# The opening of a one-core encoder step: bias rows, first squares, first two projections

## The chip, the cores and the metric

One core of one Trainium2 chip. The metric is device microseconds of one execution of the whole program; before the change three runs took 1292.07 us in the median (1292.02 to 1293.26).

## The reference, cut to what matters

One layer of a streaming encoder, for a prompt of 2048 frames with 16 meta tokens in front and for 32 new frames of a running stream. All in float32:

```
n = rmsnorm(x) * norm_g                      # mean square over 1024 columns
q, k, v, z_a, b_g, c_g, u, z_c = split(n @ w_in)      # 8 x 512 columns
s = q k / 8 + rel_bias[bucket(k_pos - q_pos)]         # 4 heads, two halves each
a = softmax(s1) - lambda * softmax(s2);  o = a @ v    # chunks of 64 frames
y = [rmsnorm(o) * silu(z_a), silu(z_c) * b_g * conv3(c_g * u)] @ w_out
out = rmsnorm(x + y)
```

The bias depends on the distance alone, so each head has one row of 383 values, of which every key window is a shifted copy.

## The kernel before, in words

Each float32 matrix product is made of three matmuls on rounded halves: `xh`/`xl` are the high and low half of a slice of x transposed (128 of the 1024 model columns by up to 560 frames), `wh`/`wl` those of the weights. A column block of 128 projected columns takes 8 slices x 3 matmuls per PSUM bank. The work runs in four passes of 512 frames; pass 0 also holds the 16 meta and 32 sample frames, 560 columns in all, so a column block needs two banks of 272 or 280 columns and 48 matmuls. Within a pass come four heads (`unit_a`: columns CQ, CK, CV, CZ, then `attend`), with the convolution columns (`unit_c`: CC, CU, CB, CG) between them; the output projection ends the program.

PSUM has eight banks: `ps_j` (tag `pj`, 2, for projections), `ps_s` (tag `s`, 3, for attention scores), `ps_t` (2) and `ps_o` (1). In pass 0 the CV block already uses banks of `ps_s`; every other block uses `ps_j`. A bank comes free when VectorE (DVE) has multiplied it by `rbs[p]` into SBUF (`ev_q`, `ev_k`, `ev_v`, `ev_z`: "evacuation" here).

`rbs[0]`, 1/rms of every frame, comes from `x_load(0)`. For each slice k it loads x (tile `g`), makes `xh[k]` on ScalarE (ACT, line 152), `xl[k]` on VectorE (line 153) and the square of the slice (tiles named `ks`, borrowed). Slices 0, 2 and 4 are squared on GpSimd (POOL, line 78, in two halves) and summed there, the other five on ScalarE (line 158) and summed on VectorE (line 162). Then a float32 matmul with a matrix of ones (line 171, `pss`) adds both sums over the partitions, in two halves of 280 frames, and `rsqrt` (lines 178 to 184) makes `rb` of each half: VectorE, two ScalarE steps, four VectorE steps.

`bias_rows` makes the bias row of each head on all 128 partitions by a matmul with a broadcast column (line 601, four of them, in `ps_j`) and a ScalarE copy (`bvec`, line 603). `prep_small` writes each to DRAM (`bd`), reads it back skewed (`g<-bd`), adds the chunk mask on VectorE (line 615), and stores it (`bz`); it also makes lambda (lines 618 to 638).

All DMAs are issued by SP in one order. A scheduler places every instruction, from its own model of times, so a change in one place moves others; each engine then runs its list strictly in that order. The order beyond the first 1300 of 7021 matmuls (about the first 140 us) is the same in both kernels.

Of the kernel before, what the change touches and what calls it, by code (L numbers as in the profile page):

```python
# [11 lines left out]
F32 = mybir.dt.float32  # L12
F32R = mybir.dt.float32r
AF = mybir.ActivationFunctionType
ALU = mybir.AluOpType
AX = mybir.AxisListType

P = 128
D = 1024
KT = D // P  # L20
# [5 lines left out]
H = 4  # L26
# [7 lines left out]
LV = WIN + P - 1  # L34
NP = (12, 6)
# [12 lines left out]
def hybrid_step(ctx: ExitStack, tc: tile.TileContext, x, xT, ckT, cv, scT, rel_bias, norm_g, w_in,  # L48
# [8 lines left out]
    pp = pool("pp", 1)  # L57
# [83 lines left out]
    def x_load(p):  # L141
        c0 = 0 if p == 0 else NX + QT * p
        tw = NX + QT if p == 0 else QT
        if p == 0:
            acc = [None, None]
        for k in range(KT):
            xt = g_tile(tw) if p == 0 else one.tile([P, QT], F32, tag="xt", name="xt", bufs=XB)
            dma(xt, xT[P * k:P * (k + 1), c0:c0 + tw])
            xh[k] = xp.tile([P, NX + QT], F32R, tag=f"xh{k}", name=f"xh{k}")
            xl[k] = xp.tile([P, NX + QT], F32R, tag=f"xl{k}", name=f"xl{k}")  # L150
            with tc.high_priority():
                S.activation(xh[k][:, :tw], xt, AF.Copy, scale=ng[:, k:k + 1])
                V.scalar_tensor_tensor(xl[k][:, :tw], xt, ng[:, k:k + 1], f32(xh[k][:, :tw]),  # L153
                                       op0=ALU.mult, op1=ALU.subtract)
            if p == 0:
                i = (1, 0, 1, 0, 1, 0, 0, 0)[k]
                sq = sqt(k, tw)
                (halved(sq, xt, xt, ALU.mult) if i else S.activation(sq, xt, AF.Square))
                if acc[i] is None:
                    acc[i] = sq  # L160
                else:
                    (G if i else V).tensor_tensor(acc[i], acc[i], sq, op=ALU.add)
        if p == 0:
            rb = one.tile([P, NX + QT], F32, tag="rb", name="rb")
            for i in range(2):
                c = slice(280 * i, 280 * (i + 1))
                var, w = (pp.tile([P, 512], F32, tag="p1", name="xv", bufs=NP[1])[:, :280] for _ in range(2))
                ps = ps_t.tile([P, 2, 256], F32, tag="pt", name="pss").rearrange("p a b -> p (a b)")[:, :280]
                parts = [a[:, c] for a in acc if a is not None]
                for j, a in enumerate(parts):  # L170
                    T.matmul(ps, lhsT=ones, rhs=a, start=(j == 0), stop=(j == len(parts) - 1))
                with tc.high_priority():
                    rsqrt(rb[:, c], ps, var, w, 1.0 / D)
            rbs[0] = rb
# [34 lines left out]
    def proj(col, p, evac):  # L209
        w2 = pre.pop((col, p), None) or w_load(col, p)  # L210
        if p > 0:
            blks = [(0, QT)]
        elif col < CK or CZ <= col < CC or col >= CG:
            blks = [(NM, 288), (288, 560)]
        else:
            blks = [(0, 280), (280, 560)]
        for b0, b1 in blks:
            if p == 0 and col == CV:
                ps = ps_s.tile([P, 512], F32, tag="s", name="pj")[:, :b1 - b0]
            else:  # L220
                ps = ps_j.tile([P, 512], F32, tag="pj", name="pj")[:, :b1 - b0]
            for k in range(KT):
                wh, wl = w2[k // 4]
                for i, (a, b) in enumerate(((wh, xh), (wh, xl), (wl, xh))):
                    T.matmul(ps, lhsT=a[:, k % 4], rhs=b[k][:, b0:b1],  # L225
                             start=(k == 0 and i == 0), stop=(k == KT - 1 and i == 2))
            evac(ps, b0, b1)


# [364 lines left out]
    def bias_rows():  # L594
        rbt = const.tile([32, H], F32, name="rbt")
        dma(rbt, rel_bias)
        oh = pp.tile([P, 512], F32, tag="p1", name="oh", bufs=NP[1])[:32, :LV]
        dma(oh, ohd)
        for h in range(H):
            pv = ps_j.tile([P, 512], F32, tag="pj", name="pv")[:, :LV]  # L600
            T.matmul(pv, lhsT=rbt[:, h:h + 1].broadcast_to([32, P]), rhs=oh, start=True, stop=True)
            bvec = pp.tile([P, 512], F32, tag="p1", name="bvec", bufs=NP[1])[:, :LV]
            S.activation(bvec, pv, AF.Copy, scale=-1.0)
            bvs.append(bvec)

    def prep_small():
        for h in range(H):
            bd = dram.tile([P, LV + 1], F32, name=f"bd{h}", tag=f"bd{h}")
            dma(bd[:, :LV], bvs[h])
            w = g_tile(512)  # L610
            G.memset(w[:, :512 - WIN], 0.0)
            src = bd[:, :]
            toep = bass.AP(tensor=src.tensor, offset=src.offset + P - 1, ap=[[LV, P], [1, WIN]])
            dma(w[:, 512 - WIN:], toep)
            V.tensor_scalar(w[:64, 448:], w[:64, 448:], -NEG, None, op0=ALU.add)
            bzd.append(dram.tile([P, 512], F32, name=f"bz{h}", tag=f"bz{h}"))
            dma(bzd[h], w)
# [195 lines left out]
```

## Time and profile before

| | |
|---|---|
| runs | 1292.02, 1292.07, 1293.26 us |
| the profiled execution | 1293.26 us, of it the span 1291.5 us |
| PE (matmul) busy | 1267.5 us, 98% |
| DVE, ACT, POOL busy | 923.9, 827.5, 699.0 us |
| mean granted clock of TensorE | 0.995 |

Busy is the sum of an engine's instructions; matmuls overlap in the records, so the distance between two starts says more than one duration. "Idle before <- X" names what ended a wait.

### The profile page before, as it was taken

How to read it: one execution, taken by the hardware profiler on the slowest of the kernel's cores; microseconds unless marked ns; L12 is line 12 of the kernel's file. 1: busy time of each engine (PE TensorE's matmuls, PEld its weight loads, DVE VectorE, ACT ScalarE, POOL GpSimd, SP SyncE). 2: the span in 40 equal slices, each digit the busy share in tenths (PEclk: the TensorE clock that was granted, in tenths of full speed). 3: DMA queues.
4: the chain of work that ended last, by engine and by line, in shares of the span. 5: the costliest groups of instructions: out<-in, count | busy, mean ns of one | idle time of the engine just before them, and what ended most of it. 6: DMA issues, size and time to landing. Idle time of an engine off the chain costs nothing.

```text
span 1291.5 us, 21630 instructions
## 1 busy us (share of the span) xinstructions
PE 1267.5 (98%) x7058; PEld 1101.4 (85%) x7058; DVE 923.9 (72%) x2086; ACT 827.5 (64%) x2030; POOL 699.0 (54%) x918
## 2 busy tenths in 40 slices
PE   8999999999999998999999999999999999999897
PEld 6999999988888886888888888888888888888675
DVE  8767566567886847787878677767786896856654
ACT  6745454675776647677767567777777786763322
POOL 5775857767565675455556555364656483432200
PEclk9999999999999999999999999999999999999999
DMA  9834444774445347444343453344334543557652
GB/s 290 226 116 129 141 112 116 216 241 149 137 117 159 125 145 228 156 137 134 101 169 124 142 177 114 116 147 119 117 109 141 177 133 124 177 181 237 215 181 81
DMA packets 108048, 198.74 MB, mean 154 GB/s; under 512 B 17408, under 2 KB 45600, under 8 KB 107936
## 3 DMA queue, kind: packets, MB, share of 16 engines
q1 hardware_dynamic: 107936, 197.37, 49.0%
q8 instruction: 55, 0.90, 0.3%
q14 instruction: 57, 0.47, 0.1%
HBM read 145.62 MB, written 43.26 MB: 146 GB/s over the span
## 4 chain that ended last, share of the span: by engine, by line
PE 55%; DVE 3%; DMA 3%; ACT 1%; issue 1%; DVEq 0%; SPq 0%; ACTq 0%
PE pj L225 27%; PE po L693 9%; PE s L446 4%; PE s L447 4%; PE pt L462 3%; PE po L469 2%; PE po L471 2%; PE po L470 2%; DMA out<-y 1%; DMA ct<-cat 1%; PE po L685 1%; DMA y<-y 0%; DVE y L731 0%; PE ptv L316 0%; DVE cs L78 0%
## 5 line engine op out<-in xcount | busy, mean ns | idle before, releaser
L78 POOL TENSOR_TENSOR wl<-wr,wh 128x256 fp32r<-128x256 f32 x480 | 377.4, 810 | 300.6 <-ACT wh L204 279.4
L225 PE MATMUL pj<-xh,wh 128*128 128x512 f32 (+2 forms) x1280 | 456.9, 358 | 3.0 <-DVE g L352 1.3
L225 PE MATMUL pj<-xl,wh 128*128 128x512 f32 (+2 forms) x1280 | 453.6, 355 | 0.9 <-DVE xl L153 0.9
L225 PE MATMUL pj<-xh,wl 128*128 128x512 f32 (+2 forms) x1280 | 452.9, 354 | 0.0
L225 PEld LDWEIGHTS pj<-xh,wh 128*128 128x128 f32 x1280 | 242.5, 190 | 34.8 <-issue 2.3
L225 PEld LDWEIGHTS pj<-xh,wl 128*128 128x128 f32 x1280 | 242.2, 189 | 29.9 <-issue 0.2
L225 PEld LDWEIGHTS pj<-xl,wh 128*128 128x128 f32 x1280 | 242.4, 189 | 29.5 <-DVE xl L153 1.4
L397 ACT ACTIVATE p<-s,nm 128x384 f32<-128x384 f32 (+5 forms) x352 | 208.6, 595 | 68.8 <-DVE nm L396 41.9
L204 ACT CAST wh<-wr 128x512 fp32r<-128x512 f32 x256 | 157.5, 618 | 102.7 <-PE pj L225 72.0
L401 DVE SCALAR_TENSOR_TENSOR p<-p,cf,p 128x384 f32<-128x384 f32 (+5 forms) x176 | 127.1, 751 | 23.9 <-ACT p L400 23.7
L396 DVE TENSOR_REDUCE nm<-s 128x1 f32<-128x384 f32 (+3 forms) x224 | 122.6, 560 | 22.7 <-PE s L447 22.5
L78 POOL TENSOR_TENSOR cll<-ct,chh 128x256 fp32r<-128x256 f32 x80 | 63.1, 815 | 131.2 <-ACT chh L671 131.2
L466 DVE TENSOR_TENSOR al<-pt,ah 128x512 fp32r<-128x512 f32 x144 | 97.2, 684 | 46.7 <-ACT ah L465 46.1
L446 PE MATMUL s<-ks,q 128*128 128x384 f32 (+5 forms) x352 | 127.3, 363 | 1.0 <-ACT p L397 0.8
L447 PE MATMUL s<-ks,q 128*128 128x384 f32 (+5 forms) x352 | 122.5, 349 | 0.0
L400 ACT ACTIVATE p<-p,cf 128x384 f32<-128x384 f32 (+5 forms) x176 | 99.1, 623 | 28.2 <-DVE cf L377 25.3
L465 ACT CAST ah<-pt 128x512 fp32r<-128x512 f32 x144 | 81.2, 585 | 42.7 <-PE pt L462 41.6
L393 DVE CUSTOM_DVE_ANT_0 s<-s,bz 128x512 f32<-128x512 f32 (+5 forms) x128 | 74.7, 588 | 21.5 <-PE s L447 19.0
L462 PE MATMUL pt<-ident,p 128*128 128x128 f32 x544 | 86.0, 272 | 0.0
L470 PE MATMUL po<-al,vh 128*128 128x256 f32 x288 | 82.5, 287 | 0.0
L469 PE MATMUL po<-ah,vh 128*128 128x256 f32 x288 | 81.7, 284 | 0.0
L471 PE MATMUL po<-ah,vl 128*128 128x256 f32 x288 | 81.2, 282 | 0.0
(237 smaller groups left out, 2192.2 us busy)
## 6 DMA issues: line engine op xcount, KB each, us to landing
wr<-in_w_in SPq DMA_DIRECT2D x128, 512.0 KB, 3.7
ct<-cat SPq DMA_DIRECT2D x28, 512.0 KB, 4.7
q<-q SPq DMA_DIRECT2D x64, 128.0 KB, 2.9
out<-y SPq DMA_DIRECT2D x32, 256.0 KB, 3.6
ks<-ksd SPq DMA_DIRECT2D x8, 776.0 KB, 5.3
xr<-in_x SPq DMA_DIRECT2D x24, 256.0 KB, 4.9
out<-g SPq DMA_DIRECT2D x24, 256.0 KB, 3.3
xt<-in_xT SPq DMA_DIRECT2D x24, 256.0 KB, 4.9
```

The source lines that it names most:

```text
L78: (engine or G).tensor_tensor(out[:, c0:c1], a[:, c0:c1], b[:, c0:c1], op=op)
L204: S.copy(wh, wi)
L225: T.matmul(ps, lhsT=a[:, k % 4], rhs=b[k][:, b0:b1], start=(k == 0 and i == 0), stop=(k == KT - 1 and i == 2))
L396: V.tensor_reduce(nm[:, c, j:j + 1], s, op=ALU.min, axis=AX.X)
L397: S.activation(pr[j][c], s, AF.Exp, bias=nm[:, c, j:j + 1], scale=-1.0, accum_out=l[:, c, j:j + 1])
L401: V.scalar_tensor_tensor(a0, a1, cf[:, 1, j:j + 1], a0, op0=ALU.mult, op1=ALU.add)
L446: T.matmul(ps, lhsT=qd[c][0][:, qs], rhs=ks[c][:, col:col + w], start=True, stop=False)
L447: T.matmul(ps, lhsT=qd[c][1][:, qs], rhs=ks[c][:, col:col + w], start=False, stop=True)
L462: T.transpose(pt[:, i, P * qi:P * (qi + 1)], cols(aa[qi], NM + P * (2 * j + i), P), ident)
L469: T.matmul(po, lhsT=vh[:, kt], rhs=ah[:, i], start=(kt == 0), stop=False)
L470: T.matmul(po, lhsT=vh[:, kt], rhs=al[:, i], start=False, stop=False)
L693: T.matmul(ps, lhsT=a[k][:, :rows], rhs=b[k], start=(k == 0 and i == 0), stop=(k == KT - 1 and i == 2))
```

## The change

Four edits. (1) The bias rows of all heads come from one matmul with the 32x4 table as the stationary operand, into one bank of `ps_s`, and one ScalarE copy of 4 partitions; that goes to a small DRAM tensor `bvd`, from which four DMAs read each row 128 times into `bd`. (2) All eight squares of pass 0 are made on ScalarE, all seven sums on VectorE, and `pss` takes one sum instead of two. (3) The first projection (CQ of pass 0) goes slice by slice over both of its banks, instead of the whole block in one bank and then the other. (4) The CK blocks of pass 0 use the score banks as CV does.

```diff
@@ x_load
-                i = (1, 0, 1, 0, 1, 0, 0, 0)[k]
                 sq = sqt(k, tw)
-                (halved(sq, xt, xt, ALU.mult) if i else S.activation(sq, xt, AF.Square))
-                if acc[i] is None:
-                    acc[i] = sq
+                S.activation(sq, xt, AF.Square)
+                if acc is None:
+                    acc = sq
                 else:
-                    (G if i else V).tensor_tensor(acc[i], acc[i], sq, op=ALU.add)
+                    V.tensor_tensor(acc, acc, sq, op=ALU.add)
...
-                parts = [a[:, c] for a in acc if a is not None]
-                for j, a in enumerate(parts):
-                    T.matmul(ps, lhsT=ones, rhs=a, start=(j == 0), stop=(j == len(parts) - 1))
+                T.matmul(ps, lhsT=ones, rhs=acc[:, c], start=True, stop=True)
@@ proj
+        spare = p == 0 and col in (CV, CK)
+        bank = lambda n: (ps_s if spare else ps_j).tile([P, 512], F32, tag="s" if spare else "pj", name="pj")[:, :n]
+
+        def step(ps, b0, b1, k):
+            wh, wl = w2[k // 4]
+            for i, (a, b) in enumerate(((wh, xh), (wh, xl), (wl, xh))):
+                T.matmul(ps, lhsT=a[:, k % 4], rhs=b[k][:, b0:b1],
+                         start=(k == 0 and i == 0), stop=(k == KT - 1 and i == 2))
+        if p == 0 and col == CQ:
+
+            pss = [bank(b1 - b0) for b0, b1 in blks]
+            for k in range(KT):
+                for ps, (b0, b1) in zip(pss, blks):
+                    step(ps, b0, b1, k)
+            for ps, (b0, b1) in zip(pss, blks):
+                evac(ps, b0, b1)
+            return
         for b0, b1 in blks:
-            if p == 0 and col == CV:
-                ps = ps_s.tile([P, 512], F32, tag="s", name="pj")[:, :b1 - b0]
-            else:
-                ps = ps_j.tile([P, 512], F32, tag="pj", name="pj")[:, :b1 - b0]
+            ps = bank(b1 - b0)
             for k in range(KT):
-                wh, wl = w2[k // 4]
...
+                step(ps, b0, b1, k)
             evac(ps, b0, b1)
@@ bias_rows
-        for h in range(H):
-            pv = ps_j.tile([P, 512], F32, tag="pj", name="pv")[:, :LV]
-            T.matmul(pv, lhsT=rbt[:, h:h + 1].broadcast_to([32, P]), rhs=oh, start=True, stop=True)
-            bvec = pp.tile([P, 512], F32, tag="p1", name="bvec", bufs=NP[1])[:, :LV]
-            S.activation(bvec, pv, AF.Copy, scale=-1.0)
-            bvs.append(bvec)
+        pv = ps_s.tile([P, 512], F32, tag="s", name="pv")[:H, :LV]
+        T.matmul(pv, lhsT=rbt, rhs=oh, start=True, stop=True)
+        bvec = pp.tile([P, 512], F32, tag="p1", name="bvec", bufs=NP[1])[:H, :LV]
+        S.activation(bvec, pv, AF.Copy, scale=-1.0)
+        bvd = dram.tile([H, LV], F32, name="bvd", tag="bvd")
+        dma(bvd, bvec)
+        bvs.extend(bvd[h] for h in range(H))
@@ prep_small
-            dma(bd[:, :LV], bvs[h])
+            dma(bd[:, :LV], bvs[h].partition_broadcast(P))
```

What the scheduler makes of it is seen at three places. In each row the line comes first (the changed file's are shifted), then the operation, what it writes and reads with buffer numbers, and the size.

The first is TensorE at its first projection matmuls (`pj` are banks, `xh`/`xl` and `wh`/`wl` the halves). Before:

```order
L225 MATMUL pj_350<-xh0_194,wh_184 128x272
L225 MATMUL pj_350<-xl0_195,wh_184 128x272
L225 MATMUL pj_350<-xh0_194,wl_185 128x272
L225 MATMUL pj_350<-xh1_206,wh_184 128x272
L225 MATMUL pj_350<-xl1_207,wh_184 128x272
```

The same place in the changed kernel:

```order
L220 MATMUL pj_336<-xh0_184,wh_174 128x272
L220 MATMUL pj_337<-xh0_184,wh_174 128x272
L220 MATMUL pj_336<-xl0_185,wh_174 128x272
L220 MATMUL pj_336<-xh0_184,wl_175 128x272
L220 MATMUL pj_337<-xl0_185,wh_174 128x272
L220 MATMUL pj_337<-xh0_184,wl_175 128x272
L220 MATMUL pj_336<-xh1_195,wh_174 128x272
```

Each slice now gives six matmuls, in two banks, before the next slice is needed.

The second is TensorE where it first needs a bank of `ps_j` again, which hangs on the evacuation of CQ. Before, after the 48 matmuls of CV (`pj_515` and `pj_541`, score banks) comes CK in `pj_431`:

```order
L225 MATMUL pj_541<-xh7_255,wh_510 128x280
L225 MATMUL pj_541<-xl7_256,wh_510 128x280
L225 MATMUL pj_541<-xh7_255,wl_511 128x280
L225 MATMUL pj_431<-xh0_194,wh_423 128x280
L225 MATMUL pj_431<-xl0_195,wh_423 128x280
```

In the changed kernel 48 matmuls of CK and the first 24 of CV (`pj_501`) stand ahead of it, and what follows is CZ with the weights `wh_588`, `wl_589`:

```order
L220 MATMUL pj_501<-xh7_243,wh_496 128x280
L220 MATMUL pj_501<-xl7_244,wh_496 128x280
L220 MATMUL pj_501<-xh7_243,wl_497 128x280
L220 MATMUL pj_598<-xh0_184,wh_588 128x272
L220 MATMUL pj_598<-xl0_185,wh_588 128x272
L220 MATMUL pj_598<-xh0_184,wl_589 128x272
```

So 24 more matmuls stand before the first that needs a bank of `ps_j`, and that one is now of the fourth column block to be loaded.

The third is VectorE at the first step of `rsqrt` (`xv<-pss`). Before, with the mask add of the first head (line 615) ahead of it and the second behind:

```order
L78 TENSOR_TENSOR wl_424<-wr_421,wh_423 128x512
L78 TENSOR_TENSOR wl_428<-wr_421,wh_427 128x512
L615 TENSOR_SCALAR g_292<-g_292 64x64
L178 TENSOR_SCALAR xv_262<-pss_264 128x280
L615 TENSOR_SCALAR g_300<-g_300 64x64
L620 TENSOR_TENSOR g_322<-g_322 128x64
```

In the changed kernel:

```order
L624 TENSOR_SCALAR g_286<-g_286 64x64
L624 TENSOR_SCALAR g_294<-g_294 64x64
L637 TENSOR_TENSOR lam2_141<-ls_312 128x1
L624 TENSOR_SCALAR g_302<-g_302 64x64
L638 TENSOR_SCALAR lam2_141<-lam2_141 128x1
L640 TENSOR_SCALAR sg_316<-lam2_141 128x1
L641 TENSOR_TENSOR sg_316<-sg_316,lam2_141 128x1
L642 RECIPROCAL sg_316<-sg_316 128x1
L643 TENSOR_SCALAR lam2_141<-lam2_141,sg_316 128x2
L646 TENSOR_TENSOR leps_142<-sg_316 128x1
L175 TENSOR_SCALAR xv_250<-pss_252 128x280
```

The mask adds of all four heads (the first one stands a little higher) and the steps of lambda now stand ahead of `rsqrt`.

On SP the store of `bvd` stands between the fifth and the sixth load of x, the weights of CK come ahead of the four `bd` copies instead of between them, and the four loads `g<-bd` stand ahead of the x rows and the weights of CZ; before, the fourth stood behind them.

## Rows read from the trace of the kernel before

**Rows 1.** The page: span, TensorE's share, the shares of the chain that ended last.
```profile
span 1291.5 us, 21630 instructions
PE 1267.5 (98%) x7058; PEld 1101.4 (85%) x7058; DVE 923.9 (72%) x2086; ACT 827.5 (64%) x2030; POOL 699.0 (54%) x918
...
PE 55%; DVE 3%; DMA 3%; ACT 1%; issue 1%; DVEq 0%; SPq 0%; ACTq 0%
```
**Rows 2.** Busy time of each engine by stretch; the columns are the stretch, its length, busy us (instructions) of PE, PEld, DVE, ACT and POOL, the granted clock, the DMA share and GB/s.
```profile
23.00:30.00 7.00, 6.60 (x50) 6.32 (x48) 6.90 (x29) 3.29 (x9) 2.12 (x4) 1.00 1.02 324
30.00:40.00 10.00, 9.74 (x77) 9.71 (x78) 4.51 (x12) 8.07 (x21) 8.75 (x16) 1.00 1.05 317
40.00:50.00 10.00, 10.00 (x80) 10.00 (x79) 7.53 (x23) 6.92 (x22) 9.11 (x13) 1.00 0.99 323
```
**Rows 3.** TensorE in order of time (start, duration, instruction, what its wait ended on): bias, first projection, `pss`, CV, the first matmul of CK.
```profile
4.09 5.89 PE L601 MATMUL pv<-oh,rbt 32*128 32x383 f32 x8 [4.09 <-DMA oh<-in_ohd]
...
10.58 0.59 PE L225 MATMUL pj<-xh,wh 128*128 128x272 f32 x1 [0.60 <-ACT bvec L603]
...
11.43 0.43 PE L225 MATMUL pj<-xh,wh 128*128 128x272 f32 x1
...
11.65 0.43 PE L225 MATMUL pj<-xl,wh 128*128 128x272 f32 x1
...
21.25 2.15 PE L171 MATMUL pss<-ks,ones 128*128 128x280 f32 x8
...
23.37 0.29 PE L225 MATMUL pj<-xl,wh 128*128 128x280 f32 x1
23.50 0.29 PE L225 MATMUL pj<-xh,wh 128*128 128x280 f32 x1
...
29.31 0.29 PE L225 MATMUL pj<-xh,wl 128*128 128x280 f32 x1
30.26 0.40 PE L225 MATMUL pj<-xh,wh 128*128 128x280 f32 x1 [0.66 <-DVE g L254]
```
**Rows 4.** VectorE in order of time: low halves, sums, weights, `rsqrt`, a mask add, lambda, the evacuation of CQ.
```profile
8.44 5.25 DVE L153 SCALAR_TENSOR_TENSOR xl<-g,ng,xh 128x560 fp32r<-128x560 f32 x4
...
18.39 0.79 DVE L153 SCALAR_TENSOR_TENSOR xl<-g,ng,xh 128x560 fp32r<-128x560 f32 x1
19.11 0.73 DVE L162 TENSOR_TENSOR ks<-ks,ks 128x560 f32<-128x560 f32 x1
19.76 0.79 DVE L153 SCALAR_TENSOR_TENSOR xl<-g,ng,xh 128x560 fp32r<-128x560 f32 x1
...
21.12 1.28 DVE L78 TENSOR_TENSOR wl<-wr,wh 128x512 fp32r<-128x512 f32 x2
...
23.00 0.43 DVE L178 TENSOR_SCALAR xv<-pss 128x280 f32<-128x280 f32 x1
23.36 0.41 DVE L615 TENSOR_SCALAR g<-g 64x64 f32<-64x64 f32 x1
...
28.00 0.15 DVE L633 RECIPROCAL sg<-sg 128x1 f32<-128x1 f32 x1
...
29.29 0.44 DVE L184 TENSOR_TENSOR rb<-rb,xv 128x280 f32<-128x280 f32 x1
29.76 0.79 DVE L254 SCALAR_TENSOR_TENSOR g<-pj,rb 128x272 f32<-128x272 f32 x2
```
**Rows 5.** ScalarE in order of time: a bias copy, the weights of CQ, a slice's high half, its square, the first step of `rsqrt`.
```profile
5.74 0.49 ACT L603 ACTIVATE bvec<-pv 128x383 f32<-128x383 f32 x1 [3.72 <-PE pv L601]
6.12 1.13 ACT L204 CAST wh<-wr 128x512 fp32r<-128x512 f32 x2
...
8.19 0.76 ACT L152 ACTIVATE xh<-g,ng 128x560 fp32r<-128x560 f32 x1
8.84 0.66 ACT L158 ACTIVATE ks<-g 128x560 f32<-128x560 f32 x1
9.40 0.75 ACT L152 ACTIVATE xh<-g,ng 128x560 fp32r<-128x560 f32 x1
...
23.47 0.44 ACT L179 ACTIVATE rb<-xv 128x280 f32<-128x280 f32 x1 [1.57 <-DVE xv L178]
```
**Rows 6.** GpSimd in order of time: squares of slices 0 and 2, then low halves of CV's weights, of q, and of CC's weights.
```profile
6.78 4.46 POOL L78 TENSOR_TENSOR ks<-g 128x280 f32<-128x280 f32 x4 [5.37 <-DMA g<-in_xT]
...
20.97 4.15 POOL L78 TENSOR_TENSOR wl<-wr,wh 128x256 fp32r<-128x256 f32 x4 [3.10 <-ACT wh L204]
30.73 3.45 POOL L78 TENSOR_TENSOR q<-g,q 64x136 fp32r<-64x136 f32 x6 [5.61 <-ACT q L259]
...
39.19 2.95 POOL L78 TENSOR_TENSOR wl<-wr,wh 128x256 fp32r<-128x256 f32 x4
```
**Rows 7.** The tile `bd` alone, between 20.25 and 20.45 us: the third load `g<-bd` (issued at 20.19), us from issue to landing.
```profile
DMA to landing us min/median/max: 3.5/3.5/3.5
```
**Rows 8.** The tile `wr` alone, between 23.6 and 23.8 us: the load of the weights of CZ (issued at 23.52), us from issue to landing.
```profile
DMA to landing us min/median/max: 6.3/6.3/6.3
```
**Rows 9.** A stall late in the program, in the output projection: the matmul that ended it, and the busy times by stretch (columns as in rows 2).
```profile
1211.19 0.50 PE L693 MATMUL po<-ks,cs 128*128 128x512 f32 x1 [2.04 <-ACT cs L671]
...
1208.00:1212.00 4.00, 1.74 (x7) 0.85 (x6) 2.53 (x7) 2.06 (x6) 0.00 (x0) 1.00 0.82 278
1212.00:1216.00 4.00, 4.00 (x11) 3.14 (x12) 2.78 (x8) 0.00 (x0) 0.00 (x0) 0.57 0.57 172
```

More of the change, by code (lines that the diff above doesn't have):

```diff
@@ L144, in x_load @@
         if p == 0:
-            acc = [None, None]
+            acc = None
         for k in range(KT):
@@ L216, in proj @@
             blks = [(0, 280), (280, 560)]
+        spare = p == 0 and col in (CV, CK)
[13 more added lines that the diff above has]
+            return
         for b0, b1 in blks:
-            if p == 0 and col == CV:
-                ps = ps_s.tile([P, 512], F32, tag="s", name="pj")[:, :b1 - b0]
-            else:
-                ps = ps_j.tile([P, 512], F32, tag="pj", name="pj")[:, :b1 - b0]
+            ps = bank(b1 - b0)
             for k in range(KT):
-                wh, wl = w2[k // 4]
-                for i, (a, b) in enumerate(((wh, xh), (wh, xl), (wl, xh))):
-                    T.matmul(ps, lhsT=a[:, k % 4], rhs=b[k][:, b0:b1],
-                             start=(k == 0 and i == 0), stop=(k == KT - 1 and i == 2))
+                step(ps, b0, b1, k)
             evac(ps, b0, b1)
```

## The prediction

> **What bounds the kernel now.** I read the page first: TensorE is busy 98% of the span and 55% of the chain that ended last [rows 1]. So the time is TensorE's work plus what it stands still. Next the stretches: from 30 us on it is full, 9.74 and 10.00 of 10 us [rows 2], so whatever is won before 30 us is kept only if the other engines can follow a TensorE that runs ahead. That makes the opening the place, and TensorE's own list shows it [rows 3]: four bias matmuls from 4.09 us, the first projection (CQ) from 10.58, `pss` at 21.25, CV until 29.31, and then a wait until 30.26 for VectorE's evacuation of CQ. Steps between starts are 0.22 us early (11.43 to 11.65) and 0.13 late (23.37 to 23.50), the first near 272 columns at 1.2 GHz, the second near 2.4.
>
> The point to compare is where TensorE first needs a bank of CQ again. Before, it gets there after 48 matmuls (CV) and goes on at **30.26** [rows 3]. In the changed order 72 stand ahead of that place. The last 46 steps before 29.31 took 5.94 us, 0.129 each [rows 3], so 24 matmuls are 3.1 us. The gain there is 30.26 + 3.1 = 33.4, less the time at which the changed kernel goes on.
>
> **Removed and added, step by step.** Three bias matmuls and three bias copies go. They cost TensorE its start: 4.09 to 9.98 us, and CQ begins at 10.58 because the copies hold its banks [rows 3]. The one left has the same 383 columns, so I give its copy the old time, 5.74 to 6.2 [rows 5]. SP now waits for that copy, to store it, before it issues the last three loads of x. ScalarE wants the sixth slice only at some 13 us, five slices of 1.21 behind the first: hidden, and it would cost nothing until the loads were 4 us late.
>
> ScalarE then does, for each slice, the high half and the square: starts 8.19, 8.84 and 9.40 give 0.65 and 0.56, 1.21 us a slice [rows 5]. VectorE does the low half and a sum: starts 18.39, 19.11 and 19.76 give 0.72 and 0.65, **1.37 us a slice**, with GpSimd idle [rows 4, 6]. Beside GpSimd's squares the first four low halves took 5.25 us, 1.31 each [rows 4]; the squares' removal buys VectorE that back, and pays for the two or three sums it takes over. VectorE is the slower of the two and sets the pace. Two weight halves at 0.64 [rows 4] from 6.8 us end at 8.1; the second low half waits for ScalarE and ends near 9.9; six more slices at 1.37 put the last low half at **18.1**, against 20.55 before [rows 4]. TensorE needs six matmuls a slice, 1.3 us at 0.22, so it keeps up at either clock level. It ends CQ near 18.6, not 21.25.
>
> Then 44 matmuls of CK, 24 of CV (four of CK fill the wait for the last slice), 68 x 0.129 = 8.8, and half of `pss`: eight records took 23.00 - 21.25 = 1.75 us [rows 3, 4], so four are 0.9. **TensorE arrives at 28.3**, or up to 1.3 later if it is still at 1.2 GHz until 21 us.
>
> **What is late next: the evacuation of CQ.** It needs `rsqrt`, and on VectorE that now stands behind four mask adds and lambda's steps. The fourth add waits for the fourth `g<-bd`. Before, the third landed at 20.19 + 3.5 = 23.7 [rows 7], with 3.09 MB queued behind the x tiles up to it (by the sizes of the tiles); the fourth now has 2.95 MB, so about 23.4. Add 0.4 for the mask add and 0.7 for six lambda steps of 0.15, which overlap a little [rows 4]: `rsqrt` starts at **24.5**, 1.5 us later than the old 23.00, though its sum is ready at 22. Before, it took 23.00 to 30.15 to the first evacuated bank [rows 4], with lambda's steps mixed in. Without them I count 0.4 + 0.45 + 0.45 (first half as far as VectorE's next turn), then 1.8 on VectorE, a second half held about 1 us by two ScalarE steps and a row of squares, four steps of 0.37 and 0.4 for the bank: 5.8. The bank is free at 30.3.
>
> **And the weights of CZ.** Before, their load was issued at 23.52 and landed 6.3 later, at 29.8 [rows 8], with time to spare, since the 48 matmuls of CK came first. Now CZ follows at once. About the same bytes go ahead of it on the one DMA queue, so I take 30.0. A cast of 0.6 [rows 5] and a GpSimd half of 0.75 to 1.0 [rows 6] follow; the first two matmuls need only the cast, the third the half: TensorE goes on in earnest at **31.4**. Gain there: 33.4 - 31.4 = **2.0 us**. Bounds: 28.3 if neither holds it (gain 5.1), and, if the `bd` copies, DRAM to DRAM and in no row here, run at half the 317 GB/s of rows 2, at which their 196 kB take 0.62 us each, 4 x 0.62 later, 33.9 (loss 0.5). I take 0.62: the queue carries loads and stores alike at that rate [rows 2].
>
> **After it.** GpSimd went from 30.73 to 42.1 through the low halves of q, of CZ's weights, of part of k and of CC's weights [rows 6]. Now it starts about as late, on CZ's, and all of k comes ahead of CC's, so these are complete near 43.8, the first of them at 41.6. TensorE, 2.0 us ahead, wants that one about 41.3: 0.3 lost.
>
> **The clock.** A stall of 2.04 us ends at 1211.19; in the next 4 us the granted clock is 0.57, after 1.00 [rows 9]. That is up to 0.43 x 4 = 1.7 us of full-speed work not done. Between 28.3 and 31.4 TensorE stands 2.5 to 3 us. I charge 0.8, half, since part of the slow spell falls into the wait.
>
> In the first projection the change alternates two banks matmul by matmul. CV did so before: its starts at 23.37 and 23.50 are in two banks, 0.13 apart at a granted clock of 1.00 [rows 2, 3]; nothing is charged.
>
> **Sum:** 2.0 - 0.3 - 0.8 = 0.9 us. The profiled execution has 1293.26 us, span 1291.5 and 1.8 around it; that is 1.2 above the median of the three runs, 1292.07. Taken from its own time this gives 1292.4, from the median **1291.2**, which I give.
>
> **The rivals.**
> 1. *No stall.* If the skewed loads land 3 us earlier (the queue ran at 317 GB/s from 30 us on [rows 2]; bursts may go faster without the copies from SBUF) and CZ's weights with them, TensorE never waits: 33.4 - 28.3 - 0.3 = 4.8, 1287.3. For it: DMA is only issued late in places. Against it: queue share 1.02 from 23 us on [rows 2].
> 2. *Slower.* The one place is `rsqrt` behind the fourth `g<-bd` in VectorE's list. Each `bd` copy is now read from DRAM, 128 times the same row, and written to DRAM. Above 1.5 us a copy (0.62 in the sum), TensorE goes on past 34.9 us, and with the 0.3 and 0.8 from above the kernel is slower by more than 0.2%; at 2.5 us it goes on at 38.9: 33.4 - 38.9 - 1.1 = -6.6, 1298.7. Against it: nothing shows DRAM as source that slow.
> 3. *The lead is not kept.* The 2 us are won, but GpSimd, 8.75 and 9.11 of 10 us busy between 30 and 50 [rows 2], hands the weights out at the old pace, and TensorE, full before, waits: 0 to 0.5, 1292.
> 4. *The whole price of the clock.* If the fall comes only as the stall ends, nothing of the slow spell is hidden: 2.0 - 0.3 - 1.7 = 0, 1292.1 [rows 9]. Against it: the wait from 29.4 to 30.26 before brought no fall, 9.74 of 10 us at 1.00 [rows 2, 3]. The Trainium skill (TensorE: Matmul & The Clock Gate, "HAM oscillation") names this mechanism, each idle stretch between bursts sending the clock back to its low level; by that rule the full price is paid, and the sum would be 1292.1.
>
> **How the numbers follow.** 0.2% is 2.6 us, about what a measurement of this kernel can tell from no change. Forecast 0.33 (own range 1289.7 to 1293.2), rival 1 0.29, rival 3 0.13, rival 2 0.13, rival 4 0.12. Faster by over 0.2% (below 1289.5): rival 1 and a little of the forecast, 0.32. Slower (above 1294.7): rival 2, and 0.02 for shifts of the schedule up to 140 us that I can't price, 0.15. Within: 0.53. The range 1287.2 to 1294.2 takes in rival 1 and the bound of doubled copies (33.4 - 33.9 - 1.1 = -1.6 from the median, 1293.7); rival 2 stays out.
>
> **What would show it.** Right: low halves 0.79 us each, the last near 18.1; `rsqrt` starts at 24 to 25 behind the fourth mask add; the first matmul of CZ starts at 30.5 to 31.5 after a wait of over 2 us; a stretch with a granted clock below 1 behind it. Wrong: `rsqrt` right after `pss` at 22 (rival 1), a `g<-bd` landing after 27 us (rival 2), or several waits of TensorE on GpSimd's `wl` between 35 and 60 us (rival 3).

## The result: slower by 0.2%, and the profile after

In 11 runs of each kernel on one chip the changed kernel has a median of 1296.12 us (1292.79 to 1297.58), the kernel before 1293.26 (1292.02 to 1295.42): ratio 1.0021, 95% interval 1.0012 to 1.0031. The medians are 2.9 us apart, slower, where 0.9 us less was forecast. The profiled execution took 1295.92 us. From the page (span, TensorE, the chain's shares), against [rows 1]:

```profile
span 1294.1 us, 21604 instructions
PE 1263.8 (98%) x7048; PEld 1099.5 (85%) x7048; DVE 919.3 (71%) x2089; ACT 827.7 (64%) x2030; POOL 683.7 (53%) x910
...
PE 56%; DVE 3%; DMA 2%; ACT 1%; issue 0%; DVEq 0%; SPq 0%; ACTq 0%
```

TensorE's busy time fell by 3.7 us, with three of four bias matmuls and half of `pss` gone, and yet the span grew by 2.6. The stretches that answer to [rows 2], with their columns, show where:

```profile
23.00:30.00 7.00, 5.92 (x46) 5.69 (x44) 5.63 (x23) 2.22 (x5) 2.81 (x4) 1.00 1.05 296
30.00:40.00 10.00, 5.70 (x23) 5.39 (x24) 6.58 (x15) 7.82 (x20) 5.46 (x10) 0.67 0.98 359
40.00:50.00 10.00, 10.00 (x81) 9.97 (x80) 3.46 (x11) 5.10 (x14) 9.12 (x15) 0.99 0.77 231
```

From 30 to 40 us TensorE starts 23 matmuls in place of 77, at a granted clock of 0.67. Its own list (start, duration, instruction, what its wait ended on), against [rows 3]:

```profile
4.23 1.43 PE L608 MATMUL pv<-oh,rbt 32*4 32x383 f32 x2 [4.23 <-DMA oh<-in_ohd]
...
8.09 0.82 PE L220 MATMUL pj<-xh,wh 128*128 128x272 f32 x2 [2.43 <-ACT xh L152]
...
28.63 0.28 PE L220 MATMUL pj<-xh,wl 128*128 128x280 f32 x1
34.30 0.60 PE L220 MATMUL pj<-xh,wh 128*128 128x272 f32 x1 [5.39 <-ACT wh L201]
...
35.51 0.43 PE L220 MATMUL pj<-xh,wh 128*128 128x272 f32 x1
35.73 0.43 PE L220 MATMUL pj<-xl,wh 128*128 128x272 f32 x1
...
47.00 0.23 PE L454 MATMUL s<-ks,q 128*128 128x144 f32 x1
...
255.27 0.47 PE L220 MATMUL pj<-xh,wh 128*128 128x512 f32 x1 [0.22 <-DVE g L360]
```

CQ starts 2.5 us earlier, the 72 matmuls are done by 28.8, and then TensorE stands for 5.4 us at the first matmul of CZ; behind it the steps are 0.22 us until 40.2. Two marks in the same list of the kernel before: the first score matmul, which has all four projections of head 0 ahead of it in both, and a matmul near 250 us, where the order is the same in both:

```profile
43.23 0.23 PE L446 MATMUL s<-ks,q 128*128 128x144 f32 x1
...
251.98 0.47 PE L225 MATMUL pj<-xh,wh 128*128 128x512 f32 x1 [0.21 <-DVE g L352]
```

The changed kernel is 3.8 us behind at the first mark and 3.3 at the second, with as many matmuls still to come in both (5243 records): in these two executions the whole loss comes from the opening. VectorE there, against [rows 4]:

```profile
17.54 0.80 DVE L153 SCALAR_TENSOR_TENSOR xl<-g,ng,xh 128x560 fp32r<-128x560 f32 x1
...
23.78 0.76 DVE L629 TENSOR_TENSOR g<-g 128x64 f32<-128x64 f32 x1 [3.58 <-DMA g<-in_lam_in]
...
25.16 0.73 DVE L624 TENSOR_SCALAR g<-g 64x64 f32<-64x64 f32 x1
...
27.77 0.44 DVE L175 TENSOR_SCALAR xv<-pss 128x280 f32<-128x280 f32 x1
...
32.80 0.45 DVE L181 TENSOR_TENSOR rb<-rb,xv 128x280 f32<-128x280 f32 x1
33.29 0.79 DVE L262 SCALAR_TENSOR_TENSOR g<-pj,rb 128x272 f32<-128x272 f32 x2
```

VectorE stands still from 20.2 to 23.8 for lambda's load, and only behind lambda and the mask adds comes `rsqrt`, at 27.77, on a sum that was ready near 23. CQ's first bank is free at 33.7, 0.4 us into the last row. ScalarE, against [rows 5], and the load of CZ's weights, issued at 27.13, against [rows 8]:

```profile
33.63 1.14 ACT L201 CAST wh<-wr 128x512 fp32r<-128x512 f32 x2 [0.55 <-DMA wr<-in_w_in]
```
```profile
DMA to landing us min/median/max: 6.4/6.4/6.4
```

The load takes as long as before, 6.4 us, but is issued 3.6 us later and lands at 33.5. So two things end within 0.6 us of the stall's end, CQ's evacuation and the cast of CZ's weights.

### The profile page after: what moved, and what is told of

Read it like the earlier page. It is cut to its first block, busy times and chain, and to the rows that moved or that the text cites. A ratio compares the mean times of both kernels' runs of the same rounds, so it can differ in the third digit from the quotient of the medians.

```text
span 1294.1 us, 21604 instructions
## 1 busy us (share of the span) xinstructions
PE 1263.8 (98%) x7048; PEld 1099.5 (85%) x7048; DVE 919.3 (71%) x2089; ACT 827.7 (64%) x2030; POOL 683.7 (53%) x910
## 4 chain that ended last, share of the span: by engine, by line
PE 56%; DVE 3%; DMA 2%; ACT 1%; issue 0%; DVEq 0%; SPq 0%; ACTq 0%
PE pj L220 27%; PE po L702 11%; PE s L454 4%; PE s L455 4%; PE pt L470 3%; PE po L477 2%; PE po L479 2%; PE po L478 2%; DMA out<-y 1%; PE po L694 1%; DVE y L740 1%; DMA ct<-cat 0%; DMA xr<-in_x 0%; PE ptv L324 0%; DVE cs L78 0%
## 5 line engine op out<-in xcount | busy, mean ns | idle before, releaser
L405 ACT ACTIVATE p<-s,nm 128x384 f32<-128x384 f32 (+5 forms) x352 | 208.4, 595 | 69.8 <-DVE nm L404 43.4
```

Of the source, the lines that this page charges most:

```text
L405: S.activation(pr[j][c], s, AF.Exp, bias=nm[:, c, j:j + 1], scale=-1.0, accum_out=l[:, c, j:j + 1])
```

## The experiments

Theory A: the loss is this stall and the 1.2 GHz behind it, and both of its causes are late through the one DMA queue. The rivals: one edit is at fault (the order of CK and CV, or the DRAM copies), the reshuffled order as such costs, or a lead can't be kept anyway. Each ratio is to the kernel before, measured on the same chip beside it. The two marks come from one profiled execution each, the ratios from 5 to 12 executions of a changed kernel. Over the 15 changed kernels of the table, lag at the second mark and ratio go together with a correlation of 0.80 and differ by 1.6 us (root mean square), so a mark of one execution is worth no more than that. Part of the scatter lies behind both marks: two stalls in the output projection near 1210 and 1225 us add up to between 2.5 and 4.3 us in all these profiles but fill's, where they make 5.8.

| run | first score matmul, us | the matmul near 250 us | ratio to before, 95% interval |
|---|---|---|---|
| before | 43.23 | 251.98 | 1 |
| changed | 47.00 | 255.27 | 1.0021 (1.0012 to 1.0031) |
| u4 | 44.96 | 253.71 | 1.0022 (1.0013 to 1.0030) |
| e234 | 45.57, with 20 matmuls fewer ahead | 255.69 | 1.0012 (1.0002 to 1.0022) |
| b1_only | 46.16 | 254.13 | 1.0010 (1.0000 to 1.0020) |
| fill | 44.73 | 254.77 | 1.0039 (1.0025 to 1.0052) |
| late | 45.47 | 258.47 | 1.0066 (1.0054 to 1.0078) |
| w_early | 43.46 | 252.33 | 1.0014 (1.0006 to 1.0023) |
| late_w_early | 47.20 | 258.57 | 1.0057 (1.0044 to 1.0070) |
| hold | 44.77 | 255.13 | 1.0012 (1.0002 to 1.0023) |
| hold_gm | 45.74 | 257.32 | 1.0021 (1.0011 to 1.0031) |
| hold_cv | 47.05 | 254.89 | 1.0003 (0.9994 to 1.0012) |
| hold_gm_cv | 45.64 | 255.05 | 1.0027 (1.0016 to 1.0038) |
| clean | 39.84 | 251.98 | 1.0007 (0.9999 to 1.0016) |
| clean2 | 39.80 | 253.91 | 1.0007 (0.9998 to 1.0017) |
| clean3 | 40.01 | 249.90 | 0.9986 (0.9975 to 0.9996) |

### One edit at a time: u4, e234, b1_only

```diff
u4     -        spare = p == 0 and col in (CV, CK)
       +        spare = p == 0 and col == CV
e234   the kernel before with the diff's x_load and proj, not its bias_rows and prep_small
b1_only  the kernel before with the diff's bias_rows and prep_small alone
```

> The changed kernel without edit 4: the CK block of head 0 goes back to the banks of ps_j, so that TensorE has 96 matmuls (CQ, CV) and no CZ ahead of the first that needs a bank of CQ again. Nothing is left out. Theory A (the loss is the wait at about 28.6 us and the 1.2 GHz that follows it; it comes from CQ's evacuation, held at 33.7 us on VectorE behind the four mask adds and lambda, and from CZ's weights, landed at 33.56): the late evacuation is still there, so TensorE still waits, at CK now, 2 to 4 us for VectorE and not for a cast, goes on at 32 to 34 us with fewer matmuls done, and the kernel is no better than the changed one: 1296 to 1298. Theory B (edit 4 is the cause, because it sets CZ ahead of its weights): 1293.3 or less. Theory C (the order of the first 140 us as such costs): no forecast, any wait near 30 us being beside the point.

> The kernel before with edits 2, 3 and 4, so the changed kernel without edit 1 (four bias matmuls and copies, stored from SBUF). Nothing is left out. Theory A: the queue still carries the same loads ahead of CZ's weights, and CQ starts near 10.5 us; TensorE still waits near 30 us for CV's or CZ's weights or for CQ's evacuation, 2 us or more: slower than before by 0.1 to 0.2%. Rival (edit 1, by its DRAM to DRAM copies, is what makes the changed kernel slow): as fast as the kernel before or faster, first score matmul at 43.2 or earlier.

> The kernel before with edit 1 alone (one bias matmul, rows stored to DRAM and read 128 times each into bd). Nothing is left out. Theory A: edit 1 alone puts the x loads and the weights of CK a little later behind the wait for the bias copy, and keeps CQ, CV, CK in the old order with 48 matmuls of CV ahead of the place that waits; TensorE starts CQ 2.5 us earlier but VectorE's pace (low halves and squares) holds it: no difference to the kernel before, within 0.1%. Rival (the DRAM to DRAM copies slow the queue and are themselves the loss): slower by 0.2% with a wait of 4 us or more near 30 us.

Without edit 4 the kernel is as slow as with it. The stall came earlier than I had said and for another load: 4.46 us at 23.41, for CV's weights. So theory B falls: the order of CK and CV only decides which late weights are met. Without edit 1 there are stalls of 1.61 us at 32.26 and of 3.10 at 39.96, the latter for a low half of weights on GpSimd; and edit 1 alone brings one of 1.79 at 25.24, again for weights. Both stand near 1.001, each interval just clear of 1 or touching it: neither part alone is shown to make the whole loss, and the intervals are too wide to divide it. Of the rivals the DRAM copies survive in part. The stretch from 16 to 18.5 us, behind their issue at 12.6 to 15.1 (columns as in [rows 2]), in the changed kernel, before, and in e234:

```profile
16.00:18.50 2.50, 2.15 (x17) 1.87 (x15) 2.50 (x5) 2.13 (x4) 0.00 (x0) 1.00 0.61 211
```
```profile
16.00:18.50 2.50, 2.50 (x15) 2.50 (x15) 2.50 (x3) 1.55 (x3) 1.87 (x2) 1.00 1.02 346
```
```profile
16.00:18.50 2.50, 2.50 (x22) 2.50 (x21) 2.50 (x4) 2.50 (x5) 0.00 (x0) 1.00 1.01 338
```

The queue moves 211 GB/s in place of 346, 0.34 MB less in 2.5 us, 1 us of its time, with its engines busy for a share of 0.61 only. The slow stretch goes with the copies: b1_only has it too (209 GB/s at 0.60), and where late, a run shown further down, issues them 2.2 us later, the same stretch is fast:

```profile
16.00:18.50 2.50, 2.15 (x17) 1.87 (x16) 2.50 (x5) 2.10 (x4) 0.00 (x0) 1.00 1.02 345
```

There it is slower from 18.5 to 21 us, 286 GB/s at 0.80. From 12 to 14 us the changed kernel's queue moved 68 GB/s in place of 239, but that is not shown to be the copies' doing: late moved 96 there, before it had issued any. Over all stretches up to 24 us the changed kernel's queue is 0.8 MB behind, 2.5 us at 317 GB/s; b1_only, with the copies, is 0.74 MB behind, e234, without them, 0.14. So edit 1 makes most of the queue's lag, and the copies' own stretch 0.34 MB of it.

### The clock: fill

```diff
+        if p == 0 and col == CZ:
+            fill = ps_o.tile([P, 512], F32, tag="po", name="fill")[:, :400]
+            for j in range(30):
+                T.matmul(fill, lhsT=last[0][:, 3], rhs=xh[7][:, :400], start=True, stop=True)
```

> The changed kernel with 30 extra matmuls of 400 columns ahead of CZ, on data already there (the last low half of CV's weights and the last slice of x), into the bank of ps_o, never read: 27 of them stand right behind the first bank of CV, where TensorE waited 5.4 us. They add work and take none away. Theory A with its clock part (TensorE that stands still is what brings the 6 us at 1.2 GHz, and these cost 2.95 us): TensorE still goes on with useful work near 34.5 us, but at full clock, and the time is about 3 us less than the changed kernel's, 1292 to 1294. Rival (the slow clock has another cause, or its cost is hidden later): 1296 or more, and the stretch from 34 to 40 us still at a granted clock near 0.5.

The clock part holds, the total does not. The stretch from 30 to 40 us:

```profile
30.00:40.00 10.00, 9.55 (x65) 9.22 (x64) 5.99 (x15) 8.43 (x21) 6.60 (x12) 1.00 1.05 386
```

Useful work goes on at 34.31, as late as in the changed kernel, but at full clock, and the first score matmul starts 2.3 us earlier, with the same work and the 30 extra matmuls done. One thing more differs, which the extra matmuls brought about in the schedule: CV's second bank now comes ahead of CZ, so the matmul at 34.31 waited for the evacuation of CK (line 294) and not for a cast:

```profile
34.31 0.39 PE L222 MATMUL pj<-xh,wh 128*128 128x280 f32 x1 [0.45 <-DVE g L294]
```

Then waits of 0.77 and 0.70 us at 46 and 50 us take 1.5 of it back, and from 250 us to the end this kernel loses 2.8 us more against the changed one in the profiled runs. Its two stalls in the output projection are 1.78 and 3.99 us (1.65 and 1.47 in the changed kernel), which is 2.65 of it; why they grew stays open.

### Taking one cause away: late, w_early, late_w_early, hold, hold_gm

```diff
late     -    prep_small()                          (behind load_small)
         +                prep_small()              (behind unit_a of head 0)
w_early  +        if (h, p) == (0, 0):              (ahead of CK's proj)
         +            for c in (CK, CV, CZ):
         +                pre[c, 0] = w_load(c, 0)
hold     +            if p == 1:                    (ahead of the load of xr; alike for kts, cvt)
         +                G.tensor_copy(xr[:, :1], rbs[0][:, 280:281])
hold_gm  hold, and: the mask adds on G in place of V, lambda's steps behind unit_a of head 0
```

> The changed kernel with the call of prep_small moved behind unit_a of head 0, so that the mask adds, the four loads g<-bd and lambda no longer stand ahead of rsqrt on VectorE, nor the g<-bd loads and lambda's load ahead of CZ's weights on SP. Nothing is left out. Theory A: rsqrt starts near 22.5 us and the first bank of CQ is free near 28.5; the weights of CZ have 0.66 MB less ahead of them, 2.1 us at 317 GB/s, and land near 31.5; TensorE goes on near 32.2 in place of 34.3, and the time is 2 us less than that of the changed kernel, 1294, or 1292.5 if the stretch at 1.2 GHz gets shorter too. Theory B (edit 4 alone, weights alone): the same, so this run does not tell A and B apart. Theory C: no difference to the changed kernel, 1296.

> The changed kernel with the loads of the weights of CK, CV and CZ of head 0 called one after the other ahead of CK's matmuls, so that CZ's are issued some 5 us or more earlier; prep_small is where it was. Nothing is left out. Theory A with both causes: CZ's weights are there by 28 us, but the g<-bd loads land up to 1.7 us later, and TensorE waits for CQ's evacuation instead, until 33.7 to 35.5 us: 1295.5 to 1297.5, no gain. If the weights are the only cause: no wait of more than 1 us, 1288 to 1290. Theory C: 1296.

> The changed kernel with both edits of the two runs before: prep_small behind unit_a of head 0, and the weights of CK, CV and CZ loaded one after the other. Nothing is left out. Theory A: neither CQ's evacuation (28.5) nor CZ's weights (27) hold TensorE for more than 1 us, no stretch at 1.2 GHz behind 28 us; TensorE is 33.4 - 29 = 4.4 us ahead of the kernel before there, and the time is 1288 to 1290, if the bias tiles that now come later (they are first needed near 45 us) don't make a wait of their own. Theory C: 1296.

> The changed kernel with the loads of kts, cvt and xr of pass 0 held back: GpSimd writes one column of each of these tiles from rb of the second half first, so that their loads cannot be issued before rsqrt is done. Nothing is left out. Theory A, now said more exactly after the runs before (the one DMA queue, full from 10 us on, carries early loads that nobody needs yet, and CZ's weights, the g<-bd loads and the xr squares that ScalarE has between its rsqrt steps all come late through it): 2.1 MB less stand ahead of CZ's weights, 6.6 us at 317 GB/s, and they land near 27; the g<-bd loads land 1.65 us earlier, rsqrt starts near 26.1 and CQ's first bank is free near 31.6. TensorE goes on near 31.7, 2.6 us earlier: 1293.5, or 1292 with a shorter 1.2 GHz stretch. Rival (the mask adds and lambda on VectorE are the whole cause, not the queue): no change, 1296.

> The run before (kts, cvt and xr held back) and in addition the four mask adds on GpSimd in place of VectorE, and lambda's part of prep_small behind unit_a of head 0. Nothing is left out. Theory A: nothing stands ahead of rsqrt any more, on VectorE, on ScalarE or in the queue; rsqrt starts near 22.5, CQ's first bank is free near 28.5, CZ's weights land by 28. TensorE waits less than 1 us there, no stretch at 1.2 GHz, and is about 4.5 us ahead of the kernel before at that point: 1288 to 1290, faster than both kernels. Rival (a TensorE that runs ahead is only stopped later, by GpSimd or the bias tiles): waits of 2 us or more between 35 and 100 us, 1291 to 1293.

Every one of these expectations failed on its numbers, and each because the wait moved to another late load. In late ScalarE's first step of `rsqrt` ran at 24.14, with nothing ahead of it, and then ScalarE stood:

```profile
24.14 0.44 ACT L176 ACTIVATE rb<-xv 128x280 f32<-128x280 f32 x1 [3.85 <-DVE xv L175]
26.69 0.63 ACT L115 ACTIVATE xr<-xr 128x512 f32<-128x512 f32 x1 [2.12 <-DMA xr<-in_x]
...
27.32 0.42 ACT L177 ACTIVATE rb<-rb 128x280 f32<-128x280 f32 x1
```

The scheduler, whose times have the load of xr earlier, had put a square of x for the next pass between the two steps. CQ's bank came free at 33.9 again and TensorE stood 4.34 us. At 53.55 VectorE, which now had the mask adds among its later work, waited 3.89 us for a `g<-bd` load, and TensorE 1.81 for it; 0.77, 0.29 and 0.65 us more were lost up to 73; this run has the largest ratio, 1.0066. Late_w_early repeats this: its square of x waited 4.58 us for its load, and TensorE stood 6.80 us, until 35.34. In w_early the loads came in a better order, but the scheduler had then set two matmuls of CV ahead of most of CK:

```profile
22.12 0.40 PE L220 MATMUL pj<-xh,wh 128*128 128x280 f32 x1 [2.78 <-ACT wh L201]
```

It is the best of these in the profile, only 0.35 us behind at 250 us, with the stall met at 22 in place of 34. The two held kernels met the same two matmuls (3.23 and 3.16 us at 22.2), which also delayed `pss` by 5 to 6 us. So theory A's reading, that one named wait is the cause, was too narrow: whichever instruction that needs a late load is set ahead of the chain holds it.

### Both causes, with TensorE's order kept: hold_cv, hold_gm_cv, clean

```diff
hold_cv, hold_gm_cv: hold or hold_gm, and ahead of CV's first bank
+            if p == 0 and col == CV and b0 == 0:
+                V.tensor_copy(ps[:, :1], sqs[0][:, :1])
clean: hold_gm_cv, and ahead of the cast of CZ's weights
+            if p == 0 and col == CZ:
+                G.tensor_copy(wh[:, 0, :1], rbs[0][:, 280:281])
```

> The run with kts, cvt and xr held back, and one addition: VectorE copies one column of the finished sum of squares into CV's first bank before CV may start, so that TensorE cannot take two matmuls of CV ahead of CK, as it did there. TensorE's first 123 matmuls now stand in the order of the changed kernel. Nothing is left out. It parts the two causes at CZ. Theory A: CZ's weights land near 25.5 us, as in the run with the loads held; the mask adds and lambda still end near 26.5 on VectorE, rsqrt starts there, CQ's first bank is free near 32.8, and TensorE, there at 28.6, waits 3.5 to 4.5 us for VectorE and not for a cast; the first score matmul starts near 45.5 (47.0 changed, 43.2 before). Weights as the only cause: no wait above 1 us, first score matmul near 42.

> The same gate on CV's first bank, with kts, cvt and xr held back, the mask adds on GpSimd and lambda behind unit_a of head 0. Nothing is left out. Theory A: pss runs near 22 us, rsqrt starts near 22.5, CQ's first bank is free near 28.5 to 29 and CZ's weights are there; TensorE waits less than 1 us, no 1.2 GHz stretch behind 28 us, the first score matmul starts near 41 (43.2 before). If the later waits of the run without the gate (0.67, 0.85 and 1.87 us at 52, 59 and 74 us) stay, 1 of these 2 us is left and the time is within 0.1% of the kernel before; if they go, 1290 to 1291. Rival (something else than these waits makes the changed kernel slow): first score matmul at 44 or later.

> The run with the gate, the held loads and GpSimd's mask adds, and one addition, since there ScalarE's list had the cast of CZ's weights, waiting for its load until 26.75 us, ahead of the first step of rsqrt, whose sum was ready at 23.2: GpSimd writes one column of CZ's high halves from rb of the second half before the casts, so that they stand behind rsqrt. Nothing is left out. Nothing that waits for a DMA now stands ahead of rsqrt on either engine. Theory A (TensorE waits near 30 us because rsqrt stands, on VectorE or ScalarE, behind something that waits for the full DMA queue): rsqrt goes from 22.7 to 27.5 without a hole, CQ's first bank is free near 28.5, TensorE waits 1 to 1.5 us (cast and low half of CZ's weights), the first score matmul starts near 41.5 (43.2 before, 47.0 changed), and the time is 1290 to 1291.5, at least 1 us below the kernel before. Rival (the wait is something else, or the lead is lost again to later waits): first score matmul at 44 or later, or a lag at 250 us of 2 us or more in spite of an early one; 1293 to 1296.

In hold_cv TensorE waits 5.84 us for VectorE, with CZ's weights landed at 27.4: evacuation alone is enough for the stall.

```profile
34.74 0.57 PE L222 MATMUL pj<-xh,wh 128*128 128x272 f32 x1 [5.84 <-DVE g L266]
```

Yet its median is level with before, 2.8 us under its own profiled run, which is its slowest. So this run speaks against theory A, unless its other executions lacked the stall, and no trace shows that. In hold_gm_cv VectorE's `rsqrt` was ready at 22.73, and ScalarE's list had the cast of CZ's weights ahead of the next step:

```profile
26.85 0.62 ACT L203 CAST wh<-wr 128x512 fp32r<-128x512 f32 x1 [4.08 <-DMA wr<-in_w_in]
27.37 0.43 ACT L178 ACTIVATE rb<-xv 128x280 f32<-128x280 f32 x1
```

So TensorE waited 5.12 us again. Clean puts that cast behind `rsqrt`, and of the wait near 30 us 1.19 us are left:

```profile
30.00 0.40 PE L224 MATMUL pj<-xh,wh 128*128 128x272 f32 x1 [1.19 <-DVE g L294]
...
39.84 0.34 PE L462 MATMUL s<-ks,q 128*128 128x144 f32 x2
...
43.38 0.50 PE L463 MATMUL s<-ks,q 128*128 128x144 f32 x2 [2.78 <-DMA q<-q]
```

The first score matmul is 3.4 us ahead of the kernel before and 7.2 ahead of the changed one. Then the second low-half copy of q, issued at 37.80 and 5.8 us under way behind the loads that I had held until then, stops TensorE for 2.78 us, the clock falls to 0.72 from 45 to 50 us, and at 250 us clean and the kernel before are level.

### Keeping the lead: clean2, clean3

```diff
clean2: for xr, and for kts and cvt of heads 1 and 2
-                G.tensor_copy(xr[:, :1], rbs[0][:, 280:281])
+                G.tensor_copy(xr[32:48, :1], f32(ms[0])[32:48, :1])
clean3: clean2, and
-                prep_lam()                         (behind unit_a of head 0)
+    prep_lam()                                     (behind prep_small)
+        G.tensor_copy(lt[:, 0, :1], rbs[0][:, 280:281])     (ahead of lambda's load)
```

> The last run with one thing moved: the loads of kts and cvt of heads 1 and 2 and of xr are held back further, until a tile (ms of head 0) is written that comes out of the transposes behind V, near 39 us, in place of rsqrt. 1.57 MB fewer stand in the queue ahead of the copies q<-q. Nothing is left out. Theory A (the full queue): the second pair of q<-q copies lands by 41 us in place of 43, TensorE stands less than 0.5 us at the first scores, no 1.2 GHz stretch behind it, 3 us of lead are left at 250 us: 1290 to 1291, some 0.2% below the kernel before. Rival (the copies themselves, or the evacuation of CQ in two blocks, hold the scores): still a wait of 2 us or more between 40 and 46 us, and 1293 to 1294.

> The last run with lambda's load and steps moved again: called before the first head, its load held until rsqrt is done (GpSimd writes one column of its tile from rb), so that it lands near 35 us and VectorE works it off in its idle time before the scores. Nothing is left out. Theory A: the wait of 2.16 us at 50.17 goes, TensorE goes on at 30 to 30.5, first score matmul near 40, no wait above 0.5 us until 60 us, and with the waits of 0.94, 0.36 and 0.96 us at 70, 90 and 93 us that the last run had (0.63 before) 1.5 to 3 us of lead are left at 250 us: 1290 to 1291.5, 0.1 to 0.2% below the kernel before. Rival (the queue still sets the pace, another late load takes the lead): a new wait of 1.5 us or more between 40 and 80 us, no lead at 250 us, 1293.

In clean2 the wait for q is gone, as theory A has it, and the next one is of my own making, VectorE behind lambda's load:

```profile
47.90 0.26 DVE L639 TENSOR_TENSOR g<-g 128x64 f32<-128x64 f32 x1 [4.03 <-DMA g<-in_lam_in]
```
```profile
50.17 0.40 PE L462 MATMUL s<-ks,q 128*128 128x272 f32 x1 [2.16 <-ACT p L413]
```

With that load in its place clean3 keeps the lead. Its `rsqrt` and CQ's evacuation on VectorE, and TensorE's marks:

```profile
22.49 0.45 DVE L177 TENSOR_SCALAR xv<-pss 128x280 f32<-128x280 f32 x1 [2.44 <-PE pss L170]
...
28.66 0.79 DVE L268 SCALAR_TENSOR_TENSOR g<-pj,rb 128x272 f32<-128x272 f32 x2
```
```profile
29.86 0.40 PE L224 MATMUL pj<-xh,wh 128*128 128x280 f32 x1 [1.16 <-DVE g L294]
...
40.01 0.23 PE L462 MATMUL s<-ks,q 128*128 128x144 f32 x1
...
249.90 0.47 PE L224 MATMUL pj<-xh,wh 128*128 128x512 f32 x1 [0.23 <-DVE g L368]
```

It is 2.1 us ahead of the kernel before at 250 us and the only one that beats it: 1291.53 us against 1293.53, ratio 0.9986 (0.9975 to 0.9996). That is 0.14%, one of 15 comparisons, with an interval just clear of 1; the lead at both marks says the same. The four edits are all in it, so what they do need not cost anything by itself; what slowed the changed kernel in its trace was waits for loads that come late, and the slow clock behind them. Two things are not shown. The additions of clean3 were not tried on the kernel before, so how much of the 0.14% is the four edits' is open. And TensorE's order is not the changed kernel's: CV's second bank (280 columns, at 29.86) comes ahead of CZ, which starts at 33.17, so CZ's weights are needed 3.3 us after TensorE goes on.

## Why the prediction was wrong

**Right.** The last low half of x ends at 18.3 us (18.1 forecast); TensorE arrives at 28.8 (28.3); from the start of `rsqrt` to the free bank it took 33.7 - 27.8 = 5.9 us (5.8, though the terms given for it add up to 6.0); no wait on GpSimd follows (0.3 had been charged).

**The step that failed first** is "About the same bytes go ahead of it on the one DMA queue, so I take 30.0". The weights of CZ landed at 33.5. Not their transfer, their issue was late, 27.13 in place of 23.52 [rows 8]. The bytes ahead were about the same, as I had said; but the queue had moved 0.8 MB less by 24 us, and SP's issues follow the landings (the one at 22.94 stood 1.1 us for CV's weights, 16.32 + 6.6). I had taken its rate for given: 317 GB/s, also for copies of which no row showed one. The bound that I kept for copies at half the rate, 33.9, was nearly the 34.30 that came: it had the queue 2.5 us behind, as it was, though the copies' own stretch made only 1 us of that.

**The same for `rsqrt`**, put at 24.5 and begun at 27.77. The fourth `g<-bd` landed at 20.99 + 4.9 = 25.9, not 23.4, and lambda's load, on which VectorE waited until 23.78, stood in no term of the sum, although its steps were in the list that I showed. So TensorE went on at 34.30 and not 31.4: the gain of 2.0 became a loss of 34.3 - 33.4 = 0.9.

**The price of the clock** was mis-sized. At the first score matmul the loss is 47.00 - 43.23 = 3.8; 0.9 of it is the stall, so 2.8 to 2.9 is the clock, charged at 0.8. I had taken half of the price of a stall of 2 us [rows 9] for a stall of 3, and kept it for the bound with a longer one. Rival 4 had the mechanism, that the fall is hardly hidden in the wait, but too small a price, 1.7: the granted clock was 0.50 from 33.5 to 40.2 us, and only 0.8 us of that lies in the wait. The Trainium skill (TensorE: Matmul & The Clock Gate, "HAM oscillation") has a wait send the clock back to its low level, so that the work behind it starts slow; the trace agrees for this stall, 0.67 from 30 to 40 us, and there was no fall in fill, where TensorE stayed busy. Not every wait does so: after 2.16 us at 50.17 in clean2 the clock stayed at 1.00.

**The sum** was +0.9 and is -3.3 at 250 us: 2.9 for the stall, 2.0 more for the clock, less the 0.3 for GpSimd and 0.4 to 0.5 that came back by 250 us (0.2 of it by waits: 0.48 and 0.15 us at 89 and 91 us that only the kernel before has, 0.42 at 152 that only the changed one has). Rival 2 had the right side and the right neighbourhood, but its sign, a `g<-bd` that lands after 27 us, was not met: the fourth landed at 25.9. The range was too narrow because its two unfavourable ends, late weights and the full clock price, were never added: a long stall brings both. Added they give 33.4 - 33.9 - 0.3 - 1.7 = -2.5. The base was low as well: three runs had a median of 1292.07, eleven have 1293.26. That 1.2 us is no part of the mechanism, and without it the range still ended at 2.1 us slower, where 2.9 came.

One thing of the change was described too widely ahead of the prediction: the conditions on `col` name head 0 alone, so edits 3 and 4 touch the first CQ and the first CK block and no other.

**Open:** why hold_cv has the stall in its profile and no loss in its median, and why fill loses 2.8 us more behind 250 us. Neither clean3 without edit 1 nor clean3's additions on the kernel before were tried.

## What to carry to other kernels

Where a queue is full, ask of the instruction that the chain needs not whether its data is early, but what stands ahead of it in its engine's list, and what load that waits for; a scheduler with optimistic load times sets such things ahead everywhere, and taking one away only shows the next. A lead on the bounding engine is worth what the loads allow: here the same four edits lost 0.2% with the loads as they fell, and a kernel with them gained 0.14% once prefetches, four mask adds, a cast and lambda's load were kept out of the way. And a stall's price can be the stall plus the slow clock behind it: here 0.9 us and 2.9.

## What the runs showed of the hardware

- Copies from DRAM to DRAM, each row read 128 times: in a stretch with them under way, 16 to 18.5 us, 211 GB/s and a busy share of 0.61 (changed) and 209 at 0.60 (b1_only), against 338 to 346 GB/s at 1.0 where the same tile came from SBUF (e234, before) and 345 at 1.02 where the copies were issued later (late). Why the engines were idle for the rest is not shown.
- After stalls of 1.16 and 1.19 us (clean3, clean) the granted clock stayed at 1.00; after one of 2.78 (clean) it was 0.82 from 43.4 to 45 and 0.72 from 45 to 50 us, and after 5.39 (changed) 0.50, the lower level, from 34.3 to 40.2, where TensorE was busy throughout. By the share not granted that is 1.7 and 2.95 us of work at the higher level.
- The length of a stall alone does not set this price: after 2.16 us (clean2, 50.17) and 1.78 us (fill, 1213.71) the clock stayed at 1.00, after 1.65 us (changed, 1213.59) it was 0.72 from 1213 to 1219.
- Early in the changed kernel the steps fell from 0.22 to 0.13 us near 13 us, with waits of 0.32 to 0.35 us between slices afterwards and no fall until 33. The profile's granted clock reads 1.00 from 8 to 13 us all the same, so there the steps show the level and the clock's row does not.
